# Token sums for a seven-product gate, formed by a lane beside the gated tiles

## The chip, the cores and the metric

The kernel runs on one core of one Trainium2 chip. The metric is the device time of one execution in microseconds, the median of several runs. All arithmetic is fp32; matmuls take each operand as a high and a low part in the fp32r format, so one exact product is three matmuls.

## The reference

A decoder block over 1040 positions (16 meta tokens, 1024 real ones), 1024 wide, one layer:

```
p     = h @ w_in + b_in          # columns: u_s5 | q | k | v | o | i | f | g_s5 | g_m
y_s5  = GLU(GELU(S5(u_s5)))      # z = gelu(y) @ s5_w_glu;  z[:, :1024] * sigmoid(z[:, 1024:])
y_m   = (o * HeadNorm(mLSTM(q, k, v, i, f))) @ m_w_out
mix   = sigmoid(g_s5) * y_s5 + sigmoid(g_m) * y_m
h     = LN(alpha * h + mix @ w_o)
h     = LN(alpha * h + relu(h @ w_up + b_up)^2 @ w_down)
```

The change concerns the two lines in the middle: the GLU product that gives `y_s5`, and the gate columns `g_m = h @ w_in[g_m] + b`, which are computed right behind it.

## The kernel before, in words

**Stages.** First come LN0 and the columns of the combined projection as a list of jobs (`q`, `v`, `o`, `u`, `g`, and two of the eight `g_m` tiles as `m0`, `m1`), with the mLSTM and the S5 scan running beside them. The last eight jobs are the **GLU tiles z0 to z7** (the gated tiles, `glu_job`, from line 910): each takes one weight tile of 128 x 1024 and makes four PSUM banks of 128 x 512, two for the gate half (evacuated by ACT with a sigmoid into `z2s`, L940) and two for the value half (evacuated by DVE, a product with the sigmoid, L944, and one with `sg`, L945). A tile is 48 matmuls of 512 columns.

Behind z7 stand the **seven-product stages** (`Seven`): the remaining six `g_m` tiles, then `m_w_out`, each computed as a 2 x 2 block product with seven multiplications instead of eight. For that the token side `h` is cut into four blocks (two halves of the 1024 features by two halves of the 1024 tokens, called 11, 12, 21, 22), and sums of blocks are needed. A block is two tiles of 128 x 1024. `raw_block` (L984 to 992) loads a block from DRAM (`h_dr`), `sub` (L1000 to 1002) subtracts two blocks on DVE, two instructions of 1024 columns, and `to_home` (L994 to 998) splits a block into its high part (ACT) and low part (DVE) inside `hT_hi` and `hT_lo`, where the matmuls read it. The first two of the seven products take blocks 11 and 21 as they stand in `hT` already; the others need sums, which `first` forms: R22 = 12 - 22, R12 = 12 - 11, R11 = 11 - R22 (the third product's block, put to its place `h01`), and R21 = 21 - R11.

**Before.** `begin()` is called when z7 starts and loads all four blocks (eight DMAs of 512 KB). `first()` is called behind z7: it loads the first three weight tiles of the gate from a ring of three buffers, splits the first one, and forms the sums. The pool of that ring is opened at z7, when the pool `mid` of the earlier stages is closed.

**Weights.** The raw tile `wraw` comes by a DMA on the SP queue; ACT copies it to `whi` (L212 for jobs, L1042 in `Seven`), DVE subtracts to get `wlo` (L213, L1043). The split of the next tile is asked for in the middle of the present one, with raised priority (`SPLIT_UP`).

**Slots.** Nearly all tiles of 128 x 1056 fp32 live in one pool of 30 slots, `big`: weights raw and split, `z2s`, the mix and gate tiles, and `rawb`, the token blocks. A tile that takes a slot waits for the last use of the tile that had it.

**Lanes.** Work that goes beside the jobs is written as generators in lanes. Each `yield x` says that the lane's next piece should come x us of matmul work later; `pump` advances all lanes while matmuls are written. One lane, `ah`, is active during the GLU tiles: `ah_scale`, then `up_early`, which forms the split sums of the first up-projection weights. `up_early` loads `wur` pairs, makes `wus` on DVE, then seven pieces `wpre` per pair, each a 512-wide ACT copy (L1412), a 512-wide DVE subtraction (L1413) and a store of 512 KB to `wu_dr` (L1414).

**What sets the order.** The framework's scheduler puts the recorded instructions of each engine in one fixed order, by a model of its own of when inputs are ready and by priority. On the chip each engine runs its list in that order, and each instruction waits for semaphores. The order around the change is therefore taken from the built programs, below.

Of the kernel before, what the change touches and what calls it, by code (L numbers as in the profile page):

```python
# [9 lines left out]
F32 = mybir.dt.float32  # L10
# [4 lines left out]
P = 128  # L15
# [4 lines left out]
META = 16  # L20
# [32 lines left out]
W5 = [2.21, 1.56, 2.6, 2.6]  # L53
Y5 = [1.97, 2.82, 3.38, 2.82]
AFT = 0
VAFT = 2
LOAD0 = "x0 x1 w0 c0 x2 w1 c1 x3 x4 w2 x5 w3 x6"
LN0_PROG = " ".join((
# [54 lines left out]
def decoder_block(  # L113
# [4 lines left out]
    nc = tc.nc  # L118
# [10 lines left out]
    def slot(name, dt=F32):  # L129
        return big.tile([P, SLOT], dt, tag="s", name=name)  # L130
# [10 lines left out]
    def row_bcast(src, n, off=0):  # L141
        return bass.AP(tensor=src.tensor, offset=src.offset + off, ap=[[0, P], [1, n]])

    lanes = {"ml": Lane(), "cv": Lane(), "s5": Lane(), "s5c": Lane(), "s5g": Lane(), "ah": Lane()}
    clock = [0.0]

    def pump(dt):
# [44 lines left out]
    ring = [None]  # L192

    def load_w(job):
        job.raw = []
        for src, n in job.loads:
            r = slot("wraw") if ring[0] is None else ring[0].tile([P, 1024], F32, tag="wr", bufs=3, name="wraw")
            nc.sync.dma_start(r[:, :n], src)
            job.raw.append(r)

# [782 lines left out]
    def s3(t):  # L983
        return t[:, :1024].rearrange("p (k s) -> p k s", k=2)  # L984

    def raw_block(dr, kh, ch, off=0):
        ts = [slot("rawb"), slot("rawb")]
        for i in range(2):
            k = 4 * kh + 2 * i
            c = off + 512 * ch  # L990
            tc.keep_in_program_order(nc.sync.dma_start(s3(ts[i]), dr[k:k + 2, :, c:c + 512].rearrange("k p s -> p k s")))  # L991
        return ts

    def to_home(ts, hm):  # L994
        hi, lo = hm
        for i in range(2):
            a_.activation(half3(hi, i), s3(ts[i]), AF.Copy)
            v_.tensor_tensor(half3(lo, i), s3(ts[i]), f32(half3(hi, i)), op=OP.subtract)

    def sub(dst, a, b):  # L1000
        for i in range(2):
            v_.tensor_tensor(dst[i][:, :1024], a[i][:, :1024], b[i][:, :1024], op=OP.subtract)  # L1002

    class Seven:
        def __init__(self, npair, wsrc, i0, p0, pieces):
# [7 lines left out]
        def load(self, i):  # L1013
            if i >= self.ntile():
                return
            r = ring[0].tile([P, 1024], F32, tag="wr", bufs=3, name="wraw")
            for j, (n, p) in enumerate(self.units[2 * i:2 * i + 2]):
                s = {5: 0, 6: 1, 7: 2, 3: 3}.get(n)
                if s is None:
                    t = self.w[self.i0 + 2 * p + (n == 4)].rearrange("p k f -> p (k f)")  # L1020
                    a = t[:, 0:512] if n == 1 else t[:, 512:1024]
                else:
                    a = ws_dr[self.p0 + p, s]
                tc.keep_in_program_order(nc.sync.dma_start(r[:, j * 512:j * 512 + 512], a))
            self.raw[i] = r
# [117 lines left out]
    def gates_and_output():  # L1143
        h00, h10, h01, h11 = home(0, 0), home(1, 0), home(0, 1), home(1, 1)
        g = Seven(3, wf, JGM + NM, 0, {1: h00, 2: h10, 6: h01, 7: h00, 4: h10, 5: h01, 3: h11})
        y = Seven(4, wmo, 0, 3, {1: h00, 2: h10, 6: h01, 7: h11, 4: h00, 5: h10, 3: h01})
        R, M = {}, {}

        def begin():
            for nm, kh, ch in (("12", 0, 1), ("22", 1, 1), ("11", 0, 0), ("21", 1, 0)):  # L1150
                R[nm] = raw_block(h_dr, kh, ch, META)

        def first():
            for i in range(3):
                g.load(i)
            g.split(0)
            sub(R["22"], R["12"], R["22"])
            sub(R["12"], R["12"], R["11"])
            sub(R["11"], R["11"], R["22"])
            to_home(R["11"], h01)  # L1160
            sub(R["21"], R["21"], R["11"])
            R.pop("11")

        def hm_load():
            for nm, kh, ch in (("11", 0, 0), ("12", 0, 1), ("22", 1, 1), ("21", 1, 0)):
                M[nm] = raw_block(hm_dr, kh, ch)

        def y_start():
            for i in range(3):
                y.load(i)  # L1170
            y.split(0)
        ghooks = {1: [lambda: to_home(R.pop("22"), h00)],
                  2: [lambda: to_home(R.pop("21"), h10)],
                  6: [lambda: to_home(R.pop("12"), h01), hm_load],
                  7: [lambda: to_home(M["11"], h00), lambda: sub(M["12"], M["12"], M["22"])],
                  4: [lambda: to_home(M["21"], h10), lambda: sub(M["11"], M["11"], M["12"])],
                  5: [lambda: to_home(M["11"], h01), lambda: sub(M["21"], M["21"], M["11"]), y_start],
                  3: [lambda: to_home(M.pop("12"), h11), lambda: sub(M["11"], M["22"], M["11"])]}
        yhooks = {1: [lambda: to_home(M.pop("21"), h00)],
                  2: [lambda: to_home(M.pop("11"), h10)],  # L1180
                  6: [lambda: to_home(M.pop("22"), h01)],
                  7: [lambda: wo_block(1, 1)],
                  4: [lambda: wo_block(0, 0)],
                  5: [lambda: wo_block(1, 0)],
                  3: [lambda: wo_block(0, 1)]}

        def run():
            g.run(lambda c, p: sdps() if c == "b" else mmps(), gate_evac, ghooks)
            y.run(lambda c, p: sdps() if c == "b" and p else mmps(), ym_evac, yhooks)
        return begin, first, run  # L1190

    def ln0_load(t):
        c0, n = rows0(t)
# [175 lines left out]
    def ah_scale():  # L1369
        gb = [slot("gB0"), slot("bB0")]  # L1370
        for i in range(2):
            nc.sync.dma_start(gb[i][:, :D], row_bcast(ln0r, D, i * D))
        rs = {}
        for t in range(9):
            if t < 8:
                rs[t] = slot("ahr")
                nc.sync.dma_start(rs[t][:, :D], ah0_dr[t * P:(t + 1) * P, :])
            if t == 0:
                yield 4.0
                for i in range(2):  # L1380
                    v_.tensor_scalar(gb[i][:, :D], gb[i][:, :D], ALPHA, None, op0=OP.mult)
                yield 2.0
                continue
            r = rs.pop(t - 1)
            for i, op in enumerate((OP.mult, OP.add)):
                v_.tensor_tensor(r[:, :D], r[:, :D], gb[i][:, :D], op=op)
                yield 1.5
            nc.sync.dma_start(ah_dr[(t - 1) * P:t * P, :], r[:, :D])

    wu_dr = dram.tile([PRE, 7, P, 1024], F32, name="wu_dr")  # L1390
# [9 lines left out]
    def up_early():  # L1400
        for p in range(PRE):
            r = [slot("wur"), slot("wur")]
            for j in range(2):
                nc.sync.dma_start(r[j][:, :D], wup[2 * p + j].rearrange("p k f -> p (k f)"))
            yield 3.0
            a11, a12, a21, a22 = r[0][:, 0:512], r[0][:, 512:1024], r[1][:, 0:512], r[1][:, 512:1024]
            n1, n2 = wsums(a11, a12, a21, a22)
            yield 3.0
            for n, w in ((1, a11), (2, a12), (3, n2[:, 0:512]), (4, a22), (5, n1[:, 0:512]), (6, n1[:, 512:1024]),
                         (7, a21)):  # L1410
                o = slot("wpre", F32R)
                a_.activation(o[:, 0:512], w, AF.Copy)  # L1412
                v_.tensor_tensor(o[:, 512:1024], w, f32(o[:, 0:512]), op=OP.subtract)  # L1413
                nc.sync.dma_start(wu_dr[p, n - 1], f32(o[:, 0:1024]))  # L1414
                yield 0.9

    for w in ORDER.split():
        n, i = w[0], int(w[1:])
# [46 lines left out]
    jobs = all_jobs  # L1465
    ws = w_sums()
    next(ws)
    begin, first, run7 = gates_and_output()

    for i, j in enumerate(jobs):  # L1470
        if j.raw is None and j.w is None:
            load_w(j)
        if j.w is None:
            split_w(j)
        if j.ran:
            next_split(jobs, i)
        for d in (1, 2):
            if i + d < len(jobs) and jobs[i + d].raw is None and jobs[i + d].w is None:
                load_w(jobs[i + d])
        if j.tag == S5_START:  # L1480
            lanes["s5c"].add(s5_pre())
        if j.tag and j.tag[0] == "o":
            while int(j.tag[1:]) not in HMREADY:
                lanes["cv"].drain()
                lanes["ml"].step()
        if j.tag == "g4":
            lanes["ah"].add(ah_scale())
            lanes["ah"].add(up_early())
        if j.tag == "z7":
            mid_ctx.close()  # L1490
            ring_ctx = ExitStack()
            ring[0] = ring_ctx.enter_context(tc.tile_pool(name="ring", bufs=1, side="left"))
            begin()
        if i >= 5 and i % 2 and ws:
            try:
                ws.send(j)
            except StopIteration:
                ws = None
        j.run(j)
        j.w = None  # L1500
# [577 lines left out]
```

## Time and profile before

| | |
|---|---|
| median of 3 runs | 1549.32 us (1548.83 to 1549.41) |
| the profiled execution | 1548.64 us, its span 1546.8 us |
| PE busy | 1508.0 us, 97% |
| DVE busy | 1080.9 us, 70% |
| ACT busy | 643.8 us, 42% |
| GpSimd busy | 97.7 us, 6% |
| mean granted clock of PE | 0.988 |
| GLU tiles z0 to z7 | about 581 to 670 us |
| seven-product stages | from 674 us |

A row of the timeline is start and duration in us, engine, line, operation, output and input tiles, sizes, count, and in brackets how long the engine had been idle just before and what ended that. The name `mm` is any PSUM bank, `gelh` and `gell` are the split GELU output that the GLU tiles read, `hT_hi` and `hT_lo` the split tokens that the gate reads. A row of the windows gives a stretch, its length, then the busy time and count of PE, PE's weight loads, DVE, ACT and GpSimd, and last the granted clock, the share of the DMA engines and GB/s.

### The profile page before, as it was taken

To read this page: it belongs to the slowest core of one execution; us is meant where nothing else is said; L and a number is where in the kernel's file an instruction comes from. 1 tells how busy PE (TensorE), PEld (TensorE's weight loads), DVE (VectorE), ACT (ScalarE), POOL (GpSimd) and SP (SyncE) were. 2 spreads that over 40 slices of the span, in tenths; PEclk is the share of its full clock that TensorE was granted. 3 is DMA by queue.
4 is the path that set the end of the run, shared out by engine and by line. 5 is a ranking of instruction groups with operands and counts; after the bars stand their busy time and mean duration, and the time that the engine had idled before them with its cause. 6 is when DMAs were issued, how large, how long until landed. Compare 5 with 4: busy or idle time off the path is not lost.

```text
span 1546.8 us, 20543 instructions
## 1 busy us (share of the span) xinstructions
PE 1508.0 (97%) x7593; PEld 1275.0 (82%) x7593; DVE 1080.9 (70%) x2083; ACT 643.8 (42%) x982; POOL 97.7 (6%) x195
## 2 busy tenths in 40 slices
PE   8999999997999999989999999999999999999996
PEld 8999998996878888868788887888888888888886
DVE  7677555659767865659688675766666689767785
ACT  6524444334354443435543243444444534433430
POOL 0000001124021200000000001000000000000000
PEclk9999999998999999999999999999999999999998
DMA  8513224413354677756272238544443897767642
GB/s 314 166 53 95 67 73 136 117 49 91 117 118 115 172 258 232 283 192 224 82 241 72 83 110 275 176 149 148 150 147 134 275 383 283 242 223 236 201 175 96
DMA packets 122149, 261.19 MB, mean 169 GB/s; under 512 B 14568, under 2 KB 36784, under 8 KB 122048
## 3 DMA queue, kind: packets, MB, share of 16 engines
q1 hardware_dynamic: 111344, 233.00, 44.1%
q0 software_dynamic: 10704, 26.88, 7.3%
q8 instruction: 60, 0.98, 0.3%
q14 instruction: 41, 0.34, 0.1%
HBM read 188.78 MB, written 84.55 MB: 177 GB/s over the span
## 4 chain that ended last, share of the span: by engine, by line
PE 30%; issue 24%; DMA 2%; DVE 1%; SPq 0%; POOL 0%; ACT 0%; POOLq 0%; DVEq 0%
PE mm L228 7%; PE mm L227 7%; PE mm L226 7%; PE sd L227 3%; PE sd L226 3%; PE sd L228 3%; DMA wpre<-wu_dr 1%; DMA rawb<-h_dr 1%; DVE wlo L1043 0%; SPq L991 0%; DMA woraw<-in_wo_dram 0%; POOL wpre L1621 0%; DVE hT_lo L1141 0%; DVE yp L1121 0%; DVE rawb L1002 0%
## 5 line engine op out<-in xcount | busy, mean ns | idle before, releaser
L226 PE MATMUL mm<-hT_hi,whi 128*128 128x512 f32 (+3 forms) x604 | 230.2, 381 | 6.3 <-ACT whi L1042 3.8
L228 PE MATMUL mm<-hT_hi,wlo 128*128 128x512 f32 (+3 forms) x604 | 226.6, 380 | 6.3 <-DVE wlo L213 3.8
L227 PE MATMUL mm<-hT_lo,whi 128*128 128x512 f32 (+3 forms) x604 | 228.4, 378 | 0.0
L228 PEld LDWEIGHTS mm<-hT_hi,wlo 128*128 128x128 f32 x604 | 114.9, 190 | 25.8 <-DVE wlo L213 4.2
L226 PEld LDWEIGHTS mm<-hT_hi,whi 128*128 128x128 f32 x604 | 115.2, 191 | 24.6 <-ACT whi L1042 4.6
L227 PEld LDWEIGHTS mm<-hT_lo,whi 128*128 128x128 f32 x604 | 115.1, 191 | 17.6 <-issue 0.4
L1777 ACT ACTIVATE dwh<-wdr 128x1024 fp32r<-128x1024 f32 x56 | 58.9, 1054 | 86.6 <-DMA wdr<-in_wdn_dram 31.0
L227 PE MATMUL sd<-dwl,dah 128*128 128x512 f32 x240 | 94.5, 394 | 0.0
L228 PE MATMUL sd<-dwh,dal 128*128 128x512 f32 x240 | 94.4, 394 | 0.0
L226 PE MATMUL sd<-dwh,dah 128*128 128x512 f32 x240 | 94.2, 393 | 0.0
L1773 ACT ACTIVATE dah<-da 128x1024 fp32r<-128x1024 f32 x56 | 58.7, 1052 | 83.6 <-PE sd L227 37.1
L1774 DVE TENSOR_TENSOR dal<-da,dah 128x1024 fp32r<-128x1024 f32 x56 | 68.2, 1219 | 24.0 <-ACT dah L1773 23.5
L228 PE MATMUL mm<-dwh,dal 128*128 128x512 f32 (+1 forms) x224 | 84.5, 378 | 0.0
L226 PE MATMUL mm<-dwh,dah 128*128 128x512 f32 (+1 forms) x224 | 84.4, 377 | 0.0
L227 PE MATMUL mm<-dwl,dah 128*128 128x512 f32 (+1 forms) x224 | 84.3, 377 | 0.0
L1778 DVE TENSOR_TENSOR dwl<-wdr,dwh 128x1024 fp32r<-128x1024 f32 x56 | 68.2, 1219 | 12.7 <-ACT dwh L1777 11.9
L213 DVE TENSOR_TENSOR wlo<-wraw,whi 128x1024 fp32r<-128x1024 f32 (+1 forms) x46 | 56.1, 1221 | 26.7 <-ACT whi L212 20.8
L226 PE MATMUL mm<-whi,hT_hi 128*128 128x256 f32 (+1 forms) x256 | 74.3, 290 | 0.0
L228 PE MATMUL mm<-whi,hT_lo 128*128 128x256 f32 (+1 forms) x256 | 74.0, 289 | 0.0
L227 PE MATMUL mm<-wlo,hT_hi 128*128 128x256 f32 (+1 forms) x256 | 73.0, 285 | 0.0
L228 PE MATMUL mm<-th,wul 128*128 128x512 f32 x156 | 61.6, 395 | 0.0
L227 PE MATMUL mm<-tl,wuh 128*128 128x512 f32 x156 | 61.5, 394 | 0.0
(474 smaller groups left out, 3688.0 us busy)
## 6 DMA issues: line engine op xcount, KB each, us to landing
da<-act_dr SPq DMA_DIRECT2D x56, 512.0 KB, 5.5
wdr<-in_wdn_dram SPq DMA_DIRECT2D x56, 512.0 KB, 6.7
wur<-in_wup_dram SPq DMA_DIRECT2D x32, 512.0 KB, 4.4
act_dr<-upy SPq DMA_DIRECT2D x64, 256.0 KB, 2.5
wraw<-in_wf_dram SPq DMA_DIRECT2D x30, 512.0 KB, 5.3
wu_dr<-wpre SPq DMA_DIRECT2D x21, 512.0 KB, 4.9
wpre<-wu_dr POOLq DMA_DIRECT2D x21, 512.0 KB, 5.1
act_dr<-upx SPq DMA_DIRECT2D x32, 256.0 KB, 3.1
```

The source lines that it names most:

```text
L213: todo.append(lambda e=v_, r=r, hi=hi, lo=lo, n=n: e.tensor_tensor(lo[:, :n], r[:, :n], f32(hi[:, :n]), op=OP.subtract))
L226: t_.matmul(ps, ah, bh, start=(i == 0 and part[0]), stop=False, skip_group_check=skip)
L227: t_.matmul(ps, ah, bl, start=False, stop=False, skip_group_check=skip)
L228: t_.matmul(ps, al, bh, start=False, stop=(i == n - 1 and part[1]), skip_group_check=skip)
L1773: a_.activation(ah[:, :D], a[:, :D], AF.Copy)
L1774: v_.tensor_tensor(alo[:, :D], a[:, :D], f32(ah[:, :D]), op=OP.subtract)
L1777: a_.activation(wh, raw[i], AF.Copy)
L1778: v_.tensor_tensor(wl, raw[i], f32(wh), op=OP.subtract)
```

## The change

`first` and `begin` are taken apart. A new generator `token_sums` runs in a lane of its own, `gp`, which is filled when z2 starts: it loads blocks 12 and 22 into slots and block 11 into a new two-buffer part of the weight ring, forms three of the four sums four us of matmul work apart, and puts the third product's block in its place in `hT`. The pool `mid` is closed and the ring is opened at z1. The ring has four weight buffers instead of three. The gate's first three weight tiles are loaded when z6 starts (`early`), block 21 when z7 starts (`begin`, which first runs the lane to its end). Behind z7 only the split of the first weight tile and the last sum are left (`first`). `sub` is now a generator that yields `GS`; where it was called as a function, `now` runs it through. To make room, the scratch memory for GpSimd's DMAs is set to 4096 bytes. `AH_START`, `AHY` and `UPY` name constants with their old values.

```diff
+AH_START = "g4"
+AHY = 1.5
+UPY = 0.9
+GY = 8.0
+GS = 4.0
...
-            r = slot("wraw") if ring[0] is None else ring[0].tile([P, 1024], F32, tag="wr", bufs=3, name="wraw")
+            r = slot("wraw")
...
-    def raw_block(dr, kh, ch, off=0):
-        ts = [slot("rawb"), slot("rawb")]
+    def raw_block(dr, kh, ch, off=0, in_ring=False):
+        ts = [ring[0].tile([P, 1024], F32, tag="rb", bufs=2, name="rawb") if in_ring else slot("rawb") for _ in range(2)]
...
     def sub(dst, a, b):
         for i in range(2):
             v_.tensor_tensor(dst[i][:, :1024], a[i][:, :1024], b[i][:, :1024], op=OP.subtract)
+            yield GS
+
+    def now(steps):
+        for _ in steps:
+            pass
...
-            r = ring[0].tile([P, 1024], F32, tag="wr", bufs=3, name="wraw")
+            r = ring[0].tile([P, 1024], F32, tag="wr", bufs=4, name="wraw")
...
+        def token_sums():
+            R["12"], R["22"] = raw_block(h_dr, 0, 1, META), raw_block(h_dr, 1, 1, META)
+            R["11"] = raw_block(h_dr, 0, 0, META, True)
+            yield GY
+            yield from sub(R["22"], R["12"], R["22"])
+            yield from sub(R["12"], R["12"], R["11"])
+            yield from sub(R["11"], R["11"], R["22"])
+            to_home(R["11"], h01)
+
         def begin():
-            for nm, kh, ch in (("12", 0, 1), ("22", 1, 1), ("11", 0, 0), ("21", 1, 0)):
-                R[nm] = raw_block(h_dr, kh, ch, META)
-
-        def first():
+            lanes["gp"].drain()
+            R["21"] = raw_block(h_dr, 1, 0, META)
+
+        def early():
             for i in range(3):
                 g.load(i)
+
+        def first():
             g.split(0)
-            sub(R["22"], R["12"], R["22"])
-            sub(R["12"], R["12"], R["11"])
-            sub(R["11"], R["11"], R["22"])
-            to_home(R["11"], h01)
-            sub(R["21"], R["21"], R["11"])
+            now(sub(R["21"], R["21"], R["11"]))
             R.pop("11")
...
-        if j.tag == "z7":
+        if j.tag == "z1":
             mid_ctx.close()
             ring_ctx = ExitStack()
             ring[0] = ring_ctx.enter_context(tc.tile_pool(name="ring", bufs=1, side="left"))
+        if j.tag == "z2":
+            lanes["gp"].add(token_sums())
+        if j.tag == "z6":
+            early()
+        if j.tag == "z7":
             begin()
...
-    nc = _bacc.Bacc("TRN2", target_bir_lowering=False, num_devices=1)
+    nc = _bacc.Bacc("TRN2", target_bir_lowering=False, num_devices=1, dynamic_dma_scratch_size=4096)
```

What this does to the order is seen at three places. In the rows that follow, numbers are the program's buffer numbers; a bracket names the queues and engines whose semaphores the instruction waits for.

ACT, from the last `wpre` copies of z1 on, before. `z2s_6081` is z2's sigmoid, `whi_6104` the next tile's (z3's) weights, and `wpre_6099` waits for PE, the end of z1's matmuls.

```order
L1412 ACTIVATE wpre_6099<-wur_6032 128x512 [waits PE_49,Pool_49]
L940 ACTIVATE z2s_6081<-mm_6082 128x512 [waits DMAHW4_49,PE_49]
L212 ACTIVATE whi_6104<-wraw_6000 128x1024 [waits DMAHW0_49,DVE_49]
L940 ACTIVATE z2s_6081<-mm_6108 128x512 [waits PE_49]
L1412 ACTIVATE wpre_6115<-wus_6057 128x512 [waits DMAHW4_49,Activation_49]
```

The same place of the change (z2's sigmoid is `z2s_6085`, z3's weights are `whi_6120`). The semaphore value of `wpre_6115` is that of z2's last use of its weights, that of the first sigmoid z2's very last matmul.

```order
L1429 ACTIVATE wpre_6115<-wur_6036 128x512 [waits PE_49]
L945 ACTIVATE z2s_6085<-mm_6086 128x512 [waits PE_49]
L945 ACTIVATE z2s_6085<-mm_6124 128x512
L217 ACTIVATE whi_6120<-wraw_6000 128x1024 [waits DMAHW2_49,DMAHW7_49,DMAHW0_49,DVE_49]
L1429 ACTIVATE wpre_6131<-wus_6061 128x512 [waits DVE_49]
```

The copy into the slot of a weight tile has moved from the end of z1 to the end of z2, the two sigmoids stand together behind it, and the split of the next weights behind both.

DVE at the same place, before: z3's `wlo` (`wlo_6105`) and z2's evacuations (`z2s_6081`).

```order
L1413 TENSOR_TENSOR wpre_6099<-wur_6032,wpre_6099 128x512 [waits Activation_49]
L213 TENSOR_TENSOR wlo_6105<-wraw_6000,whi_6104 128x1024 [waits DMAHW0_49,DMAHW7_49,DVE_49,Activation_49]
L1413 TENSOR_TENSOR wpre_6115<-wus_6057,wpre_6115 128x512 [waits DMAHW4_49,Activation_49]
L1413 TENSOR_TENSOR wpre_6125<-wur_6033,wpre_6125 128x512 [waits Activation_49]
L944 TENSOR_TENSOR z2s_6081<-mm_6130,z2s_6081 128x512 [waits PE_49]
```

The same place of the change: z3's `wlo` is `wlo_6121`, `rawb_6101` and `rawb_6102` are the first sum, and `mm_6169` is z2's last bank.

```order
L1007 TENSOR_TENSOR rawb_6101<-rawb_6097,rawb_6101 128x1024 [waits DMAHW7_49,DMAHW5_49,DVE_49]
L1430 TENSOR_TENSOR wpre_6115<-wur_6036,wpre_6115 128x512 [waits Activation_49]
L949 TENSOR_TENSOR z2s_6085<-mm_6146,z2s_6085 128x512 [waits Activation_49]
L1007 TENSOR_TENSOR rawb_6102<-rawb_6098,rawb_6102 128x1024 [waits DMAHW6_49,DMAHW4_49,DMAHW0_49]
L949 TENSOR_TENSOR z2s_6085<-mm_6169,z2s_6085 128x512 [waits Activation_49]
L950 TENSOR_TENSOR sgs_5178<-z2s_6085,sgs_5178 128x512 [waits DVE_49]
L1007 TENSOR_TENSOR rawb_6097<-rawb_6097,rawb_6105 128x1024 [waits DMAHW1_49,Pool_49]
L950 TENSOR_TENSOR sgs_5178<-z2s_6085,sgs_5178 128x512 [waits DVE_49]
L1007 TENSOR_TENSOR rawb_6098<-rawb_6098,rawb_6106 128x1024 [waits DMAHW2_49]
L218 TENSOR_TENSOR wlo_6121<-wraw_6000,whi_6120 128x1024 [waits DMAHW3_49,Activation_49]
```

`wlo` has moved behind the evacuation of z2's last bank and three of the sums' instructions. On PE, z3 to z7 now each begin with eight matmuls on `whi` before the first on `wlo`; before, at z3, two did.

SP and then ACT around the end of z4 in the change: the piece `wpre_6271` and its store, z6's raw weights (`wraw_6278`), z4's sigmoid (`z2s_6280`) and z5's weights (`whi_6303`).

```order
L1431 DMA wu_dr_104<-wpre_6248 128x1024 [waits DMAHW4_49,DVE_49]
L1431 DMA wu_dr_104<-wpre_6261 128x1024 [waits DMAHW5_49,DVE_49]
L203 DMA wraw_6278<-in_wglu_dram 128x1024 [waits PE_49]
L1431 DMA wu_dr_104<-wpre_6271 128x1024 [waits DMAHW7_49,DVE_49]
L1431 DMA wu_dr_104<-wpre_6288 128x1024 [waits DMAHW0_49,DVE_49]
L1431 DMA wu_dr_104<-wpre_6298 128x1024 [waits DMAHW1_49,DVE_49]
```

```order
L1429 ACTIVATE wpre_6288<-wur_6187 128x512 [waits DMAHW2_49,DVE_49]
L1429 ACTIVATE wpre_6298<-wus_6221 128x512 [waits DMAHW3_49,PE_49]
L945 ACTIVATE z2s_6280<-mm_6281 128x512 [waits DMAHW5_49]
L945 ACTIVATE z2s_6280<-mm_6307 128x512
L217 ACTIVATE whi_6303<-wraw_6193 128x1024 [waits DMAHW7_49,DMAHW3_49]
```

The load waits for z4's last use of its `whi`; `whi_6303` waits for the store of `wpre_6271`, whose slot it takes. In the order before, the weights of z5 stand between the two sigmoids of z4.

More of the change, by code (lines that the diff above doesn't have):

```diff
@@ L142, in row_bcast @@
         return bass.AP(tensor=src.tensor, offset=src.offset + off, ap=[[0, P], [1, n]])
-    lanes = {"ml": Lane(), "cv": Lane(), "s5": Lane(), "s5c": Lane(), "s5g": Lane(), "ah": Lane()}
+    lanes = {"ml": Lane(), "cv": Lane(), "s5": Lane(), "s5c": Lane(), "s5g": Lane(), "ah": Lane(), "gp": Lane()}
     clock = [0.0]
@@ L1174, in gates_and_output @@
                   6: [lambda: to_home(R.pop("12"), h01), hm_load],
[L1175 to L1178, printed above, removed]
+                  7: [lambda: to_home(M["11"], h00), lambda: now(sub(M["12"], M["12"], M["22"]))],
+                  4: [lambda: to_home(M["21"], h10), lambda: now(sub(M["11"], M["11"], M["12"]))],
+                  5: [lambda: to_home(M["11"], h01), lambda: now(sub(M["21"], M["21"], M["11"])), y_start],
+                  3: [lambda: to_home(M.pop("12"), h11), lambda: now(sub(M["11"], M["22"], M["11"]))]}
         yhooks = {1: [lambda: to_home(M.pop("21"), h00)],
@@ L1189, in run @@
             y.run(lambda c, p: sdps() if c == "b" and p else mmps(), ym_evac, yhooks)
-        return begin, first, run
+        return token_sums, early, begin, first, run
     def ln0_load(t):
@@ L1386, in ah_scale @@
                 v_.tensor_tensor(r[:, :D], r[:, :D], gb[i][:, :D], op=op)
-                yield 1.5
+                yield AHY
             nc.sync.dma_start(ah_dr[(t - 1) * P:t * P, :], r[:, :D])
@@ L1414, in up_early @@
                 nc.sync.dma_start(wu_dr[p, n - 1], f32(o[:, 0:1024]))
-                yield 0.9
+                yield UPY
     for w in ORDER.split():
@@ L1467, in decoder_block @@
     next(ws)
-    begin, first, run7 = gates_and_output()
+    token_sums, early, begin, first, run7 = gates_and_output()
     for i, j in enumerate(jobs):
@@ L1485, in decoder_block @@
                 lanes["ml"].step()
-        if j.tag == "g4":
+        if j.tag == AH_START:
             lanes["ah"].add(ah_scale())
             lanes["ah"].add(up_early())
-        if j.tag == "z7":
+        if j.tag == "z1":
             mid_ctx.close()
```

## The prediction

> **What bounds the kernel now.** TensorE (PE) is busy 97% of the span on the page, so I asked first who makes it wait between 570 and 830 us, where the change works, and then read its timeline around the one place that the answer gives, the passage from the last GLU tile, z7, to the first gate product.
>
> ```profile
> PE mm L226 <- ACT whi L1042: 3.8, 1, 3.8
> PE mm L228 <- DVE wlo L1043: 2.4, 1, 2.4
> ...
> 669.33 0.40 PE L227 MATMUL mm<-gell,whi 128*128 128x512 f32 x1
> 669.56 0.40 PE L228 MATMUL mm<-gelh,wlo 128*128 128x512 f32 x1
> 673.74 0.50 PE L226 MATMUL mm<-hT_hi,whi 128*128 128x512 f32 x1 [3.79 <-ACT whi L1042]
> ...
> 677.71 0.80 PE L228 MATMUL mm<-hT_hi,wlo 128*128 128x512 f32 x1 [2.36 <-DVE wlo L1043]
> ...
> 680.44 0.63 PE L228 MATMUL mm<-hT_hi,wlo 128*128 128x512 f32 x1
> 680.87 0.53 PE L226 MATMUL mm<-hT_hi,whi 128*128 128x512 f32 x1
> ...
> 681.93 0.39 PE L226 MATMUL mm<-hT_hi,whi 128*128 128x512 f32 x1
> ```
>
> Matmuls follow each other every 0.23 us before the passage and every 0.43 us behind it (680.44 to 680.87). The one at 681.93 is the sixteenth after z7's last; at the full pace it would start at 669.56 + 16 x 0.23 = 673.24. **The passage costs 8.7 us**, two waits and a slow stretch. The windows show the slow stretch as a lower granted clock (the last three numbers of a row are clock, DMA share and GB/s), and that the GLU tiles ahead of it have no wait at all: PE is busy in all of 11.0 us, DVE (VectorE) in 6.4 to 9.2.
>
> ```profile
> 603.00:614.00 11.00, 11.00 (x49) 8.93 (x48) 9.21 (x15) 5.36 (x9) 0.00 (x0) 1.00 0.53 198
> 614.00:625.00 11.00, 11.00 (x49) 8.91 (x48) 6.39 (x11) 3.24 (x6) 0.00 (x0) 1.00 0.87 295
> 658.70:669.80 11.10, 11.10 (x49) 8.79 (x47) 6.41 (x7) 1.20 (x2) 0.00 (x0) 1.00 1.03 370
> 669.80:682.00 12.20, 6.06 (x17) 4.24 (x17) 10.13 (x11) 3.27 (x4) 0.00 (x0) 0.72 0.44 157
> ...
> 679.00:680.00 1.00, 1.00 (x3) 0.72 (x3) 0.93 (x1) 0.00 (x0) 0.00 (x0) 0.50 0.76 293
> ...
> 681.00:682.00 1.00, 1.00 (x6) 0.83 (x5) 0.00 (x0) 0.10 (x1) 0.00 (x0) 0.92 0.00 0
> ```
>
> The queue says why: eight token blocks are loaded from 654.26, the gate's weights only from 661.73, and DVE and ACT (ScalarE) begin when these land.
>
> ```profile
> 606.23 7.69 SPq L1414 DMA_DIRECT2D wu_dr<-wpre  x6
> ...
> 654.26 6.58 SPq L991 DMA_DIRECT2D rawb<-h_dr  x8
> 661.73 7.10 SPq L1024 DMA_DIRECT2D wraw<-in_wf_dram  x6
> ...
> 664.50 3.95 DVE L1002 TENSOR_TENSOR rawb<-rawb 128x1024 f32<-128x1024 f32 x3 [4.14 <-DMA rawb<-h_dr]
> ...
> 672.63 1.06 ACT L1042 ACTIVATE whi<-wraw 128x1024 fp32r<-128x1024 f32 x1 [1.36 <-DMA wraw<-in_wf_dram]
> ```
>
> **The change part by part.** *The passage.* The weights are now loaded at z6 and split inside z7, and the sums that stood ahead of them are done long before. The order of the changed ACT and DVE streams puts the first `whi` and `wlo` of the gate between z7's own evacuations, so nothing is left to wait for: minus 8.7 us.
>
> *The GLU tiles pay.* Every tile's split weights, the `wpre` pieces of the early up weights, and now four token blocks share 30 slots. Already before, ACT waited for slots:
>
> ```profile
> 603.19 0.63 ACT L1412 ACTIVATE wpre<-wur 128x512 fp32r<-128x512 f32 x1 [3.28 <-PE mm L227]
> ...
> 609.39 0.62 ACT L1412 ACTIVATE wpre<-wus 128x512 fp32r<-128x512 f32 x1
> 609.91 0.62 ACT L1412 ACTIVATE wpre<-wur 128x512 fp32r<-128x512 f32 x1
> ...
> 624.67 0.63 ACT L1412 ACTIVATE wpre<-wur 128x512 fp32r<-128x512 f32 x1 [3.54 <-DMA wu_dr<-wpre]
> ...
> 631.29 1.06 ACT L212 ACTIVATE whi<-wraw 128x1024 fp32r<-128x1024 f32 x1 [1.91 <-DMA wu_dr<-wpre]
> ```
>
> The first of these waited for the end of z1's matmuls, the other two for a store of an earlier piece; none reached PE, because the next tile's weights still came in time (the third is itself the `whi` of z5, and PE shows no wait there). In the changed order such waits stand ahead of the next tile's `whi` on ACT, and `wlo` comes behind the old tile's last evacuation on DVE. The next tile can then begin only after the old one has ended. Steps: 0.52 us from one 512-wide ACT copy to the next (609.39 to 609.91), 1.05 for a 1024-wide one; on DVE 0.60 and 1.14:
>
> ```profile
> 614.46 0.69 DVE L944 TENSOR_TENSOR z2s<-mm,z2s 128x512 f32<-128x512 f32 x1 [0.28 <-PE mm L228]
> 615.07 0.68 DVE L1413 TENSOR_TENSOR wpre<-wur,wpre 128x512 fp32r<-128x512 f32 x1
> ...
> 632.54 1.23 DVE L213 TENSOR_TENSOR wlo<-wraw,whi 128x1024 fp32r<-128x1024 f32 x1 [2.65 <-ACT whi L212]
> ...
> 672.44 1.21 DVE L1002 TENSOR_TENSOR rawb<-rawb 128x1024 f32<-128x1024 f32 x1
> 673.57 1.22 DVE L998 TENSOR_TENSOR hT_lo<-rawb,hT_hi 128x1024 fp32r<-128x1024 f32 x1
> ```
>
> z3. T is the end of z2. ACT's second `wpre` waits for it, then come two sigmoids and `whi`: T + 0.1 + 3 x 0.52 + 1.05 = T + 2.7. PE has 8 matmuls on `whi` (1.85 us) and needs `wlo`, which on DVE follows the `wpre` piece, four 0.60 operations of z2 and three sums: T + 0.8 + 5 x 0.60 + 3 x 1.14 + 1.22 = T + 8.4. Lost: 8.4 - 1.85 = 6.6 us. The first sum stands ahead of all this on DVE and waits for its loads, which SP issues behind the store of 606.23, 0.8 us apart (eight in 6.58). z2 ended at about 614.2 (the multiplication at 614.46 waited for it), so a sum that starts by 613.9 costs nothing. The third load, the one it needs, goes out near 608.6, and the shortest landing of such a block is 5.9 (below): 614.5. Before, from the first load to the first sum, 10.2 us passed (654.26 to 664.50): 607.0 + 10.2 = 617.2. That adds 0.6 to 3.3 us, or nothing if it lands sooner; I take 0.6, as the queue is half as busy here (DMA share 0.53 against 1.03), and **7.2** for z3 (6.6 to 9.9).
>
> z4. A is the end of z3's `wlo`. Its `whi` waits behind two stores in a row, because one piece takes the slot of another that must first be stored. Landing times of such stores, of stores of that size that go out singly (`ah_dr`), and of token blocks:
>
> ```profile
> DMA to landing us min/median/max: 2.6/4.9/7.8
> ...
> ah_dr<-ahr SPq DMA_DIRECT2D x8, 512.0 KB, 3.0
> ...
> DMA to landing us min/median/max: 5.9/9.3/10.9
> ```
>
> I take 3.0, because here a store goes out alone while the 4.9 comes from bursts of six or seven (bounds 2.6 and 4.9). DVE reaches the second piece at A + 4 x 1.14 + 3 x 0.60 + 0.68 = A + 7.0; its store lands at A + 10.1; two sigmoids and `whi` make A + 12.3. PE has 40 matmuls, to A + 9.2. Lost: **3.1** (2.7 to 6.0, there with the first store late as well).
>
> z5. Its `whi` waits for a store that SP can issue only behind a weight load, and that load takes the slot of z4's `whi`, free when z4 ends: two issues 0.6, landing 3.0, plus 1.4 for the 512 KB ahead (at the 370 GB/s above), `whi` 1.1: **6.1** (4.3 to 6.6, with 2.6 and 4.9 for both transfers in all).
>
> z6 and z7. The sigmoids of z5 take a slot that its own weights' end frees: 0.1 + 2 x 0.52 + 1.05 = 2.2, and 0.3 more for `wlo`: **2.5** (2.2 to 2.5). At z7 two `wpre` copies stand ahead of the same: **3.3**.
>
> Sum of the waits: 7.2 + 3.1 + 6.1 + 2.5 + 3.3 = 22.2 us; with the bounds 19.1 to 28.3.
>
> *The clock.* After the waits of 3.79 and 2.36 us PE ran at 0.50 until about 681.1 (0.92 in the window from 681), 3.4 us from 677.71, in which half of the work was lost: 1.7 us. Elsewhere a stretch with PE busy in 0.71 of 2 us kept the full clock, one with 0.47 of 2 was followed by 0.50:
>
> ```profile
> 339.00:341.00 2.00, 0.71 (x4) 0.52 (x4) 1.47 (x8) 1.29 (x6) 0.00 (x0) 1.00 0.01 4
> ...
> 455.00:457.00 2.00, 0.47 (x3) 0.06 (x1) 1.42 (x9) 0.80 (x3) 0.00 (x0) 1.00 0.00 0
> ...
> 460.00:461.00 1.00, 1.00 (x4) 0.82 (x3) 0.08 (x1) 1.00 (x2) 0.00 (x0) 0.50 0.83 279
> ```
>
> So each of the five stalls may cost 0 to 2.4 us (12 matmuls at 0.43). That of z3 is hidden, since z4 waits for stores anyway. z5's is longer than the one that lowered the clock: 1.7. Those of z4, z6 and z7 (2.5 to 3.3) lie between the two cases, half of 1.7 each: 4.3 in all (0 to 9.6 for four).
>
> [...]
>
> *The rest at nothing.* A fourth weight buffer and the sums' new places free DVE at the passage, which is already free of waits. The smaller scratch of the GpSimd DMAs could only slow that queue, whose `wpre` loads go out one every 2.8 us because buffers come free at that pace (913.63, 916.38 below), so they are covered; uncovered, 21 landings of 5.1 us would be the ceiling.
>
> ```profile
> 913.63 0.53 POOL wpre L1621
> 914.16 2.21 issue
> 916.38 0.52 POOL wpre L1621
> ...
> wpre<-wu_dr POOLq DMA_DIRECT2D x21, 512.0 KB, 5.1
> ```
>
> Behind the passage both kernels run the same PE work with no wait in the answer quoted first, so nothing gives the loss back. Net: 22.2 + 4.3 - 8.7 = **+17.8 us**, made against the profiled execution (span 1546.8, its time 1548.64): 1548.64 + 17.8 = 1566.4. The median of the runs is 0.7 above that execution (1549.32), so **1567 us**.
>
> **The rivals.** *The tiles cover it* (faster). DVE has 1.8 to 4.6 us free in each tile and PE no wait; if the slots were free early enough, only the gain would be left: 1549.3 - 8.7 = 1540.6. It decides as long as all five stalls together stay below 8.7 us. Against it stands the wait for a tile's own last matmul, which no earlier landing removes: z3, z6 and z7 alone make at least 6.6 + 2.2 + 3.3 = 12.1. Chance 0.06.
>
> *Only z3 is pinched* (no change). If the slots have recovered by z4, 7.2 + 1.7 of clock against 8.7 leaves 1549.5. For it: before, two waits for stores passed unseen. Against it: the order keeps `wlo` behind the last evacuation in all five. Chance 0.05.
>
> *Slow stores* (slower still). With landings of 7.8 instead of 4.9 (two in a row at z4, one at z5: 8.7 more), the first sum at 617.2 and the clock lost at four stalls: 28.3 + 8.7 + 9.6 - 8.7 = 38, 1587. For it: the token loads now share the queue with the stores. Chance 0.09.
>
> **How the numbers follow.** The forecast has 0.80. Its bounds are 19.1 - 8.7 = +10.4 and 28.3 + 9.6 - 8.7 = +29.2, 1560 to 1578; I widen these to 1557 for a stall that is partly covered and to 1580 for the nearer part of the slow stores. What a measurement can tell from no change is 0.2%, 3 us: faster 0.06, the same 0.04, slower 0.90.
>
> **What would show it.** Right: PE waits for ACT `whi` (now L217) and DVE `wlo` (L218) at four or five tile boundaries between 614 and 690, the longest at z3 and z5; a granted clock of 0.5 behind some of them; no wait at the gate's first product (L1052 and L1053 in the changed lines); the same PE time behind it. Wrong step by step: the ACT copy that waits for z2's end standing elsewhere than at 614, z5's `whi` not released by a store, or a wait left at the passage. The forecast falls if the five boundaries show no waits, or if ones worth over 9 us turn up in stages that the change does not touch.

## The result, and the profile after

The changed kernel takes **1565.76 us** (median of four runs, 1562.89 to 1567.65) against 1549.37 before: 1.0104 times as long, with a 95% interval of 1.0086 to 1.0122. It is slower by 16.4 us; the forecast was 1567, in a range from 1557 to 1580.

The waits of PE between 560 and 720 us in the profile of the changed kernel (total, times, longest):

```profile
PE mm L231 <- ACT whi L217: 16.3, 5, 7.4
PE mm L233 <- DVE wlo L218: 3.7, 1, 3.7
```

Both waits of the passage from z7 to the gate are gone, and five tiles now wait for their weights' high part, one of them for the low part as well. PE's timeline shows where: for z3 to z7, the last matmul of the tile before and the first one that waited, and last the passage.

```profile
615.46 0.40 PE L233 MATMUL mm<-gelh,wlo 128*128 128x512 f32 x1
618.88 0.50 PE L231 MATMUL mm<-gelh,whi 128*128 128x512 f32 x1 [3.02 <-ACT whi L217]
...
624.73 0.80 PE L233 MATMUL mm<-gelh,wlo 128*128 128x512 f32 x1 [3.74 <-DVE wlo L218]
...
635.27 0.40 PE L233 MATMUL mm<-gelh,wlo 128*128 128x512 f32 x1
636.77 0.50 PE L231 MATMUL mm<-gelh,whi 128*128 128x512 f32 x1 [1.10 <-ACT whi L217]
...
639.00 0.50 PE L233 MATMUL mm<-gelh,wlo 128*128 128x512 f32 x1
...
648.11 0.40 PE L233 MATMUL mm<-gelh,wlo 128*128 128x512 f32 x1
655.87 0.80 PE L231 MATMUL mm<-gelh,whi 128*128 128x512 f32 x1 [7.36 <-ACT whi L217]
...
669.63 0.40 PE L233 MATMUL mm<-gelh,wlo 128*128 128x512 f32 x1
671.91 0.55 PE L231 MATMUL mm<-gelh,whi 128*128 128x512 f32 x1 [1.88 <-ACT whi L217]
...
684.44 0.40 PE L233 MATMUL mm<-gelh,wlo 128*128 128x512 f32 x1
687.76 0.50 PE L231 MATMUL mm<-gelh,whi 128*128 128x512 f32 x1 [2.92 <-ACT whi L217]
...
700.27 0.39 PE L233 MATMUL mm<-gelh,wlo 128*128 128x512 f32 x1
700.50 0.39 PE L231 MATMUL mm<-hT_hi,whi 128*128 128x512 f32 x1
```

At the full pace matmuls start 0.231 us apart (before, from 582 to 669.7 us, 379 of them with a median step of 0.231), and a tile has 48. The loss of a tile is read in two parts: the stall (z3 and z4 up to the ninth matmul, the first on `wlo`; z5 to z7 up to the first), and what the rest of the tile took beyond the full pace, which is the clock.

| tile | stall, forecast | stall, measured | clock, forecast | clock, measured |
|---|---|---|---|---|
| z3 | 7.2 | 624.73 - 615.46 - 9 x 0.231 = 7.2 | 0 (hidden in z4's) | 1.5 |
| z4 | 3.1 | 639.00 - 635.27 - 9 x 0.231 = 1.65 | 0.85 | 0.1 |
| z5 | 6.1 | 655.87 - 648.11 - 0.23 = 7.5 | 1.7 | 2.9 |
| z6 | 2.5 | 2.05 | 0.85 | 1.7 |
| z7 | 3.3 | 3.1 | 0.85 | 1.7 |
| sum | 22.2 | 21.5 | 4.3 | 7.9 |

The gate now starts 0.23 us behind z7, so the 8.7 us are gained in full. Net on this stretch: 21.5 + 7.9 - 8.7 = 20.7 us. The span grew by 18.8 (1565.6 against 1546.8). The rest lies outside the stretch. z0's first sigmoid already starts 1.4 us later than before (591.68 against 590.24 us, rows below), ahead of the edited stages. Nearly all of this lag is there within the first 17 us of the program: the first long row of matmuls (94 of them) starts at 16.24 us against 14.88, and from 10 to 15 us the granted clock is 0.50 against 0.71. Runs of one kernel differ by more than that: the fourteen of the kernel before that stand beside the run scratch took 1547.31 to 1551.87 us. The program's end behind the last store is 3.3 us shorter, which turned out to be a part of the change (the runs scratch and scratch8k, below). 20.7 + 1.4 - 3.3 = 18.8. The sigmoid's row in ACT's timeline before:

```profile
590.24 0.60 ACT L940 ACTIVATE z2s<-mm 128x512 f32<-128x512 f32 x1 [7.13 <-issue]
```

and in the changed kernel's:

```profile
591.68 0.60 ACT L945 ACTIVATE z2s<-mm 128x512 f32<-128x512 f32 x1 [7.17 <-issue]
```

Who was late, at z3: rows of ACT and DVE in the timeline of the changed kernel.

```profile
615.66 0.63 ACT L1429 ACTIVATE wpre<-wur 128x512 fp32r<-128x512 f32 x1 [14.32 <-PE mm L232]
615.91 1.23 DVE L1007 TENSOR_TENSOR rawb<-rawb 128x1024 f32<-128x1024 f32 x1 [7.67 <-DMA rawb<-h_dr]
...
617.77 1.06 ACT L217 ACTIVATE whi<-wraw 128x1024 fp32r<-128x1024 f32 x1 [0.51 <-DVE wpre L1430]
...
623.46 1.22 DVE L218 TENSOR_TENSOR wlo<-wraw,whi 128x1024 fp32r<-128x1024 f32 x1
```

At z5, rows of SP's queue and of ACT:

```profile
648.31 0.33 SPq L203 DMA_DIRECT2D wraw<-in_wglu_dram  x1
648.98 2.31 SPq L1431 DMA_DIRECT2D wu_dr<-wpre  x3
...
654.76 1.06 ACT L217 ACTIVATE whi<-wraw 128x1024 fp32r<-128x1024 f32 x1 [3.12 <-DMA wu_dr<-wpre]
```

ACT idles 14.3 us until z2's matmuls give a slot back, then makes two sigmoids and z3's `whi`; DVE has waited 7.7 us for the first token blocks and reaches `wlo` behind the sums and evacuations. In the trace its ten instructions from 615.91 to 623.46 have the order listed for the change. At z5 the `whi` waits for a store that SP issued at 648.98, behind the load that z4's end released.

### The profile page after: what moved, and what is told of

It is laid out like the page before. It is cut to its first block, busy times and chain, and to the rows that moved or that the text cites. A ratio compares the mean times of both kernels' runs of the same rounds, so it can differ in the third digit from the quotient of the medians.

```text
span 1565.6 us, 20536 instructions
## 1 busy us (share of the span) xinstructions
PE 1516.5 (97%) x7593; PEld 1279.9 (82%) x7593; DVE 1081.4 (69%) x2083; ACT 643.3 (41%) x982; POOL 98.6 (6%) x195
## 4 chain that ended last, share of the span: by engine, by line
PE 74%; issue 16%; DVE 5%; DMA 2%; ACT 2%; SPq 0%; POOLq 0%; DVEq 0%; ACTq 0%
PE mm L231 18%; PE mm L232 18%; PE mm L233 18%; PE sd L232 3%; PE sd L233 3%; PE sd L231 3%; PE mm L1322 2%; PE mm L1330 1%; PE pu L482 1%; PE pn L478 1%; PE pn L479 1%; DMA wiB<-wrow_dr 1%; DMA wu_dr<-wpre 1%; PE ln L1278 0%; PE s5y L863 0%
## 5 line engine op out<-in xcount | busy, mean ns | idle before, releaser
L231 PE MATMUL mm<-gelh,whi 128*128 128x512 f32 x128 | 54.1, 423 | 16.3 <-ACT whi L217 16.3
```

Source lines behind the costliest of these rows:

```text
L231: t_.matmul(ps, ah, bh, start=(i == 0 and part[0]), stop=False, skip_group_check=skip)
```

## The experiments

Two theories were put against each other. **Slots:** the four tiles of the blocks 12 and 22 take 4 of 30 slots from z2 on (these are the "four token blocks" of the prediction; block 11 lies in the ring), and what waits for slots stands ahead of the next tile's weights. **The lane's own work:** its six loads, its six subtractions and the splitting of block 11 hold up the queue and DVE. Each run is built anew, and the order on the engines is made anew with it, so a run shows what its edit costs together with the order that follows from it.

**Four slots held and nothing else (hold4).** On the kernel before:

```diff
+        if j.tag == "z2":
+            HOLD = [slot("hold") for _ in range(4)]
+            for h in HOLD:
+                g_.memset(h[0:1, 0:1], 0.0)
         if j.tag == "z7":
+            for h in HOLD:
+                g_.tensor_copy(h[0:1, 0:1], f32(j.w[0][0][0:1, 0:1]))
```

> The kernel before with four slots of the pool taken from z2 until z7 starts, and nothing else of the change: no token loads, no sums, weights of the gate loaded as before. Theory of the slots: the four slots alone make the waits at the starts of z3 to z7 (some 18 to 22 us of waits, the longest again at z5) while the passage from z7 to the gate keeps its two waits, so 1568 to 1582 us. Theory of the lane's own work (sums on DVE, loads in the queue): without them nothing waits between z2 and z7, and the time stays within 2 us of 1549.

Measured: 1576.66 us, 1.0185 of before (1.0167 to 1.0203), 28 us more. The waits of PE from 560 to 760 us:

```profile
PE mm L226 <- ACT whi L212: 16.8, 5, 6.8
PE mm L226 <- ACT whi L1042: 4.6, 1, 4.6
PE mm L228 <- DVE wlo L1043: 2.8, 1, 2.8
PE mm L228 <- DVE wlo L213: 0.3, 1, 0.3
```

No token was loaded and nothing summed ahead of z7, yet five waits for `whi` are there, 16.8 us against 16.3 in the change. Four held slots make the stalls, and the passage keeps its own waits besides. What is missing is the wait for `wlo` at z3.

**One slot more (big31).** In the change, `bufs=30` of the pool `big` becomes 31.

> The change with 31 slots in the pool instead of 30. Theory of the slots: one slot more lets ACT copy the wpre pieces and the next tile's weights earlier, at least half of the 21.5 us of waits goes, 1548 to 1558 us. Theory of the lane's own work: loads and sums are the same, 1563 to 1568 us.

Measured: 1549.48 us, 1.0004 of before (0.9995 to 1.0014): one slot of 4224 bytes per partition gives back 16 us, with the same lane, loads and sums. The waits that stay:

```profile
PE mm L231 <- ACT whi L217: 7.4, 4, 2.4
PE mm L233 <- DVE wlo L218: 0.7, 1, 0.7
```

8.1 us instead of 20.0, none over 2.4. The wait for `wlo` at z3 is gone too, although the sums are unchanged: in the order of this build `wlo` (615.78) stands behind one of the six subtractions, in the change (623.46) behind four. Whether the slot moved it there, or the scheduler's order would have changed in any case, is not separated by this run.

**The change without the lane's subtractions (nosub).**

```diff
-            yield from sub(R["22"], R["12"], R["22"])
-            yield from sub(R["12"], R["12"], R["11"])
-            yield from sub(R["11"], R["11"], R["22"])
+            yield GS
```

> The change without the six subtractions of the lane (blocks are loaded, hold their slots and block 11 is put in its place unsubtracted; the gate's third, fourth and sixth products then have the wrong token side). Theory of the slots: the 3.7 us wait for wlo at z3 goes and most of the other waits stay, 1554 to 1564 us. Theory of the lane's own work: with the sums gone the tiles follow without waits and only the gain at the passage is left, 1539 to 1544 us.

Measured: 1560.48 us, 1.0079 of before (1.0064 to 1.0095), some 4 to 5 us less than the change. The waits for `whi` stay, only that for `wlo` at z3 goes:

```profile
PE mm L231 <- ACT whi L217: 16.6, 5, 8.0
PE mm L233 <- DVE wlo L218: 0.3, 1, 0.3
```

**Two slots held (hold2).** As hold4, with `range(2)`.

> As the run with four held slots, but two. Four held slots cost 28 us, one slot given back in the change saved 16. If the cost went by the number of slots, two would cost about half of four: 1562 us. If the pool has some slack, so that the first slots taken only meet waits that PE does not see, and the last ones make each tile begin behind the old one: at most one wait of 1 to 2 us at the starts of z3 to z7 and a passage lengthened by some us, 1550 to 1556 us.

Measured: 1554.3 us, 1.0033 of before (1.0020 to 1.0046). Two slots cost 4.5 us, four cost 28. The waits:

```profile
PE mm L226 <- ACT whi L1042: 7.6, 1, 7.6
PE mm L228 <- DVE wlo L1043: 1.6, 1, 1.6
PE mm L226 <- ACT whi L212: 0.9, 1, 0.9
```

One tile waits 0.9 us; most of the cost has moved to the passage, whose wait for `whi` doubled. So the pool had about two slots of slack over the tiles, and the third and fourth slot together cost some five times what the first two did.

**The lane started at z6 (lane_z6).** `if j.tag == "z2"` ahead of `token_sums` becomes `"z6"`.

> The change with the lane started at z6 instead of z2; all else as in the change. If the slots held through z2 to z6 make the loss, it is gone while most of the gain at the passage and the 3.4 us at the program's end stay: 1539 to 1546 us, no wait at z3 to z6. If the lane's loads and sums make the loss wherever they stand, they now fall on z6 and z7: waits of 4 us and more at z7 and the gate, 1550 to 1558 us.

Measured: 1541.79 us, 0.9960 of before (0.9946 to 0.9974). No wait at z3 to z7; 3.8 us in two waits for `wlo` inside the gate. With the lane's work done late the tiles run as before. Together with hold4 this says that what hurts is how long the slots are held.

**The change without the lane (early).**

```diff
 def begin():
-    lanes["gp"].drain()
-    R["21"] = raw_block(h_dr, 1, 0, META)
+    for nm, kh, ch in (("12", 0, 1), ("22", 1, 1), ("11", 0, 0), ("21", 1, 0)):
+        R[nm] = raw_block(h_dr, kh, ch, META)
...
-        if j.tag == "z2":
-            lanes["gp"].add(token_sums())
```

with the four sums in `first` behind `g.split(0)`, as before.

> The change without the lane: the four blocks are loaded when z7 starts and summed behind z7, as before; the ring is opened at z1, has four weight buffers, the gate's first three weight tiles are loaded at z6, the scratch is 4096 bytes. If the passage was slow because the weights came late, as the prediction has it: 1540 to 1543 us, no wait between z2 and the gate. If the sums ahead of the weights' low parts on DVE are as much the cause: waits of 1 to 3 us for wlo at the gate's second and third weight tile, 1544 to 1548 us. In either case no wait at z3 to z7; a wait there would speak for the ring or the scratch as a cause.

Measured: 1541.79 us, 0.9955 of before (0.9941 to 0.9970). No wait at z3 to z7. The time alone would fit the first theory, but about 3.5 us of the gain belong to the program's end, and the trace shows the second: PE waits 1.33 and 2.02 us for `wlo` in the gate. DVE's rows there, from `early`:

```profile
675.45 2.35 DVE L1007 TENSOR_TENSOR rawb<-rawb 128x1024 f32<-128x1024 f32 x2
677.72 1.22 DVE L1053 TENSOR_TENSOR wlo<-wraw,whi 128x1024 fp32r<-128x1024 f32 x1
...
683.40 2.35 DVE L1003 TENSOR_TENSOR hT_lo<-rawb,hT_hi 128x1024 fp32r<-128x1024 f32 x2
685.67 1.22 DVE L1053 TENSOR_TENSOR wlo<-wraw,whi 128x1024 fp32r<-128x1024 f32 x1
```

The second and third low parts stand behind sums and copies that are needed only later. Early weights alone remove the wait for `whi`, not those for `wlo`.

**The gate's weights loaded late again (noearly).** In the change, `early()` is called in `first` instead of at z6.

> The change with the gate's first three weight tiles loaded behind z7 (in first), as before, instead of at z6. If the early loads make the gain at the passage, as the prediction has it: two waits for whi and wlo return there, some 6 to 9 us on the changed kernel's time, 1571 to 1575 us. If the sums made ahead are enough (the queue then holds two token loads ahead of the weights instead of eight, and DVE is free): no wait at the passage, 1562 to 1568 us.

Measured: 1565.31 us, 1.0098 of before (1.0084 to 1.0112), the same as the change, and no wait at the passage. Rows of SP and ACT:

```profile
684.64 2.02 SPq L996 DMA_DIRECT2D rawb<-h_dr  x2
686.71 3.74 SPq L1034 DMA_DIRECT2D wraw<-in_wf_dram  x6
...
693.74 1.06 ACT L1052 ACTIVATE whi<-wraw 128x1024 fp32r<-128x1024 f32 x1 [1.74 <-DMA wraw<-in_wf_dram]
```

With two token loads ahead of the weights instead of eight, these go out at 686.71 and the first `whi` is made at 693.74; z7's last matmul starts at 697.90. Once the lane has moved six token loads and six subtractions, loading the weights at z6 adds nothing.

**Three splits ahead of the sums (split3z5 and min5).** If the passage needs early weights and free DVE time only for three low parts, no token block has to be held at all. On `early`, split3z5 loads the weights at z5 and splits three tiles first; min5 does it on the kernel before, without the fourth ring buffer and the smaller scratch:

```diff
-        if j.tag == "z7":
+        if j.tag == "z5":
             mid_ctx.close()
             ring_ctx = ExitStack()
             ring[0] = ring_ctx.enter_context(tc.tile_pool(name="ring", bufs=1, side="left"))
+            early()
+        if j.tag == "z7":
             begin()
...
-        def first():
+        def early():
             for i in range(3):
                 g.load(i)
-            g.split(0)
+
+        def first():
+            for i in range(3):
+                g.split(i)
```

`split` then skips a tile that is split already, and in min5 the jobs' own raw tiles stay in slots (`r = slot("wraw")`), as in the change.

> The change without the lane (as the run early), with two more edits: the gate's first three weight tiles are loaded at z5 instead of z6, and all three are split in first, ahead of the sums. If the 4.3 us that the run early still loses behind z7 come only from the sums standing ahead of the second and third wlo on DVE: no wait from z2 to the end of the gate's first three tiles, 8 to 9 us less than before, 1539 to 1541 us. If DVE is simply short of time there, the waits move to a later weight tile and the time stays at 1541 to 1543 us.

> The kernel before with the smallest edit that follows from the runs so far: the ring (three buffers, as before) is opened at z5, the gate's first three weight tiles are loaded there, and all three are split behind z7 ahead of the sums; the token blocks are loaded at z7 and summed behind it as before; no lane, no fourth buffer, no smaller scratch. If order and early weights are all that matters: within 1 us of the run that has the fourth buffer and the scratch as well, 1539 to 1542 us. If the fourth buffer is needed: a wait for the fourth weight tile and 1542 to 1546 us.

Measured: split3z5 **1537.69 us**, 0.9919 of before (0.9906 to 0.9931), and min5 1541.22 us, 0.9943 (0.9930 to 0.9957). In neither does PE wait at all from 575 to 760 us. The low parts on DVE in split3z5:

```profile
667.91 1.22 DVE L1053 TENSOR_TENSOR wlo<-wraw,whi 128x1024 fp32r<-128x1024 f32 x1
...
673.65 1.22 DVE L1053 TENSOR_TENSOR wlo<-wraw,whi 128x1024 fp32r<-128x1024 f32 x1
```

The first and the third of the three are shown; all are made by 674.9. Two instructions of the sums run ahead of the first (663.83 and 665.22), the rest between and behind them. min5 gains 8.3 us, close to the whole 8.7 of the passage. split3z5 lies 3.5 us below min5, not within 1 us as expected, and below the 1539 us expected of it; the smaller scratch alone gains 3.5 us, as the next runs show. split3z5 beats both kernels of this study, by 12 and 28 us.

**The scratch alone (scratch, scratch8k).** The kernel before with `dynamic_dma_scratch_size=4096`, and with 8192.

> The kernel before with the scratch memory of the GpSimd DMAs at 4096 bytes and nothing else. Costed at nothing in the prediction: within 1 us of before. If the smaller ring held back that queue, the 21 wpre loads and the weight sums would come later: up to 21 landings of 5.1 us, at the least some us more than before.

> The kernel before with the scratch memory of the GpSimd DMAs at 8192 bytes. In the trace GpSimd's last instruction (a drain) takes 6.50 us with the scratch as before and 2.91 us with 4096 bytes. If its length goes with the size of that memory (before has 16384 bytes by the room that the smaller one set free): about 4.1 us, the program's end 2.4 us earlier, 1546 to 1548 us. If the drain is merely shorter when the ring is below some size, or the difference has another cause: 2.9 or 6.5 us again.

Measured: 1545.96 us, 0.9978 of before (0.9968 to 0.9988), with 4096 bytes; 1547.20 us, 0.9987 (0.9978 to 0.9996), with 8192. Not nothing, as costed, but a gain. The span and the last store in the timeline of the kernel before:

```profile
core 0 of [0], span 1546.8 us
...
1540.69 0.33 SPq L1890 DMA_DIRECT2D out_dram<-arow  x1
```

and the same with 4096 bytes of scratch:

```profile
core 0 of [0], span 1543.9 us
...
1541.14 0.33 SPq L1890 DMA_DIRECT2D out_dram<-arow  x1
```

From the last store's issue to the end it is 6.1 us before and 2.8 in scratch. The trace's own records, which the views leave out, name the instruction: GpSimd's closing drain takes 6.50 us before and 2.91 in the changed kernel, and the end follows the last store's issue by 6.08 and 2.77 us. With 8192 bytes the time is 2.6 us below the 1549.82 measured for before beside it (0.6 to 3.4 by the interval); 2.4 was expected. That fits a drain that grows in proportion to the scratch, but the interval is too wide to show it. Seven kernels with 4096 bytes (the change, scratch, big31, nosub, early, noearly, split3z5) end 2.7 to 2.8 us behind the issue of their last store; before, hold4 and min5 end 6.1 behind it.

## Why the prediction was right, and where it was not

**The bound and the passage.** That the change works where PE never idles but at the passage, and that 8.7 us are to be had there: right, z7 and the gate now run without a gap, and min5 gains 8.3 by that alone. The cause was given as two moves together. Noearly shows that the moved sums and loads suffice without the early weights, and split3z5 and min5 that early weights suffice if three splits go ahead of the sums.

**Slots as the mechanism.** Right, and shown: hold4 makes the waits for `whi` without the lane, big31 takes 16 us away with it, nosub leaves them in place. That `wlo` stands behind the sums costs only at z3 (3.7 us of wait, gone in nosub).

**z3.** 7.2 forecast, 7.2 measured. The first sum started at 615.91, 0.2 us behind the end of z2's matmuls (615.69), where 0.3 behind it was forecast.

**z4 and z3's clock.** 3.1 forecast, 1.65 measured, and 1.5 of clock at z3 where none was counted, "since z4 waits for stores anyway". Together 3.15: the stores came when forecast, and the slower z3 used up the wait.

**z5: a mis-sized term.** 6.1 forecast with 3.0 for the landing of the store and 1.4 for the load ahead of it; from the store's issue at 648.98 to `whi` at 654.76 it took 5.8 instead of 4.4. The stall measured 7.5, outside the bounds of 4.3 to 6.6. The store itself landed after 5.7 us. The 3.0 for a store alone was not the mistake; the landings of all stores of this line in the changed kernel are:

```profile
DMA to landing us min/median/max: 2.6/2.9/6.4
```

By the trace's records those that had no load issued on the queue in the 3 us ahead of them took 2.6 to 3.0 us, those that had one 5.5 to 6.4. So the 1.4 for the 512 KB ahead was too little: here it was 2.7. Two more stores follow this one within 2 us (the row of three above); whether they have a share is not separated.

**z6 and z7.** 2.5 and 3.3 forecast, 2.05 and 3.1 measured.

**The clock: a mis-sized term.** 4.3 forecast (0 to 9.6), 7.9 measured with z3's, 6.4 without. z5's 2.9 lies above the 2.4 given as the most for one stall, since the clock stayed at 0.50 until 661.98, 6.1 us behind the end of the wait. The 12 matmuls of that most were the author's estimate; in z5 fourteen started 0.42 us or more apart. "Half of 1.7" for z6 and z7 was a choice between two cases; both fell (1.7 us each). The last section has the windows.

**The scratch: the step that failed.** "The smaller scratch of the GpSimd DMAs could only slow that queue" was an assumption, and looked at the transfers and not at the end of the program. The 21 `wpre` loads land after a median of 5.1 us in before and in scratch alike; the run scratch measures a gain of 3.5 us.

The two misses have opposite signs: stalls and clock came out 2.9 us dearer than forecast in the profiled execution (29.4 against 26.5), the program's end 3.3 us cheaper. The forecast of 1567 is nearer to 1565.76 than its parts deserve. The four runs also spread over 4.8 us, those before over 1.2. The two profiles differ by 1.4 us already ahead of the edited stages, as said of z0's first sigmoid; what makes the rest of the spread was not shown.

**The rivals.** That the tiles cover the loss needed stalls below 8.7 us in all, and they were 21.5. That only z3 is pinched fell with z5. Slow stores held for z5 alone.

## What to carry to other kernels

Before a buffer is taken earlier, count how long it will be held and what else turns over in the same pool: here two held slots of 30 cost 4.5 us and four cost 28, though the only work added was two one-element GpSimd instructions for each slot. Ask first which few instructions the stalled stage really needs early. Three weight tiles loaded early and split ahead of the sums gave nearly the whole gain, with no token block held. And read the program's last microseconds in the trace as a stage of its own.

## What the runs showed of the hardware

**In the GLU tiles and the gate the granted clock followed the work of the window before.** In the two profiles, before and after, each change of the clock lies on a grid of 3.41 us, and in ten profiles cut on such a grid (before, the change, hold4, big31, nosub, early, lane_z6, hold2, noearly, scratch) each window from 590 to 720 us has a clock of 1.00 or 0.50. The rows are windows on that grid in the changed kernel (length, PE's busy time and count, PE's weight loads, DVE, ACT, GpSimd, granted clock, DMA share, GB/s):

```profile
614.19:617.61 3.42, 1.67 (x8) 1.01 (x6) 1.70 (x2) 1.60 (x3) 0.00 (x0) 1.00 1.05 396
...
621.02:624.43 3.41, 0.00 (x0) 0.00 (x0) 3.41 (x4) 0.63 (x1) 0.00 (x0) 1.00 0.00 0
624.43:627.85 3.42, 3.12 (x7) 2.51 (x8) 3.42 (x5) 2.48 (x4) 0.00 (x0) 0.50 0.18 73
...
655.15:658.57 3.42, 2.70 (x6) 2.15 (x7) 2.52 (x3) 1.93 (x3) 0.00 (x0) 0.50 0.30 113
658.57:661.98 3.41, 3.41 (x9) 2.64 (x8) 0.00 (x0) 0.00 (x0) 0.00 (x0) 0.50 0.88 309
661.98:665.39 3.41, 3.41 (x16) 2.78 (x15) 0.00 (x0) 0.00 (x0) 0.00 (x0) 1.00 0.69 278
668.81:672.22 3.41, 1.53 (x7) 0.94 (x6) 1.76 (x3) 2.03 (x3) 0.00 (x0) 1.00 0.00 0
672.22:675.63 3.41, 3.41 (x9) 2.64 (x8) 2.62 (x4) 0.63 (x1) 0.00 (x0) 0.50 0.00 0
```

A window with 1.53 us of PE work is followed by half the clock, one with 1.67 by the full one. For a window at half the clock the author takes half of the busy time as its work, an estimate: 2.70 (worth 1.35) is followed by half again, 3.41 (worth 1.71) by full. So counted, in the ten profiles between 590 and 720 us the windows followed by 0.50 have at most 1.53 us of work in 3.41 (the change), those followed by 1.00 at least 1.50 (big31). PE did not have to idle through a window to lose the next: 1.88 us in the one from 668.81 were enough, and the lost window cost z6 1.7. All this holds for this stretch alone. Earlier in the program, with smaller matmuls (128x128 to 128x400), windows with more work were followed by 0.50 too: the one from 455.87 us of the kernel before has 1.98 us of PE's busy time, the one from 371.85 of the changed kernel 1.82. What the clock counts is therefore not the busy time as such, and stays open. Where the grid fell mattered as well. In noearly z6 waited 1.89 us as in the change (1.88), but across the border of two windows, and lost nothing:

```profile
666.37:669.79 3.42, 2.26 (x10) 1.50 (x8) 2.14 (x5) 1.36 (x3) 0.00 (x0) 1.00 0.02 8
669.79:673.20 3.41, 2.39 (x9) 1.71 (x10) 2.98 (x4) 0.97 (x2) 0.00 (x0) 1.00 0.00 0
```

**The program's end got shorter with a smaller scratch.** GpSimd's closing drain took 6.50 us with the default scratch (before) and 2.91 with 4096 bytes (the change); the runs with 8192 and 4096 bytes alone took 2.6 and 3.5 us less than before. Below 4096 the author expects nothing more here, since in the changed kernel SP's own last wait, behind the last store (until 1564.73 us), already ends later than the drain (1564.53); smaller sizes were not run.
